# Row normalisation: another dealing of 64 KiB row chunks to partitions, in groups of four

## Chip, cores, metric

One core of a Trainium2 chip. The metric is device time in microseconds. Before: 82.85 us (median of the six runs, 82.76 to 83.07; the first three alone gave 82.86). Differences here, e12's apart, are about 1% or less, so the argument rests on the packet records of the traces (start, duration and size of every DMA packet) as much as on times.

## The reference

```python
def setup_inputs():
    batch, dim = 1024, 4096
    return {"x": np.random.randn(batch, dim).astype(np.float32), "axis": -1, "eps": np.float32(1e-12)}

def reference(x, axis, eps):
    norm = np.sqrt(np.sum(x ** 2, axis=axis, keepdims=True) + eps)
    return (x / norm).astype(np.float32)
```

16.8 MB are read and 16.8 MB written; every row is divided by its length.

## The kernel before

Two tiles of 128 partitions; each partition holds four whole rows, 64 KiB in one piece. Both loads are issued at once (at 0.00 and 0.80 us in the trace), the first even ahead of the program's opening barrier. Each tile's rows are squared into scratch, summed to norms, then scaled in place, and the tile is stored as one transfer.

```python
    R = 4
    # ... assert cut ...
    n_tiles = N // (P * R)                                            # 2
    x_t = x.rearrange("(t p r) d -> t p (r d)", p=P, r=R)
    out_t = out_flat.rearrange("(t p r) d -> t p (r d)", p=P, r=R)
    # ... pools, eps, scratch cut ...
    for i in range(n_tiles):
        g = RowGroups(nc, io, stats, scratch, D, R, eps_t)
        load = nc.sync.dma_start(out=g.flat(), in_=x_t[i])
        if i == 0:
            first_load_to_front(nc, load.ins)
        groups.append(g)

    for i, g in enumerate(groups):
        g.square_dve(R - 1)
        # ... squares, norms and scales of the four rows, cut ...
        g.square_act(2)
        g.norm(2)
        g.scale(2)
        store = nc.sync.dma_start(out=out_t[i], in_=g.flat())
    one_barrier_behind_last_store(nc, store.ins)
```

Of the kernel before, what the change touches and what calls it, by code (L numbers as in the profile page):

```python
# [1 line left out]

# [4 lines left out]


ACT_F = mybir.ActivationFunctionType
ALU = mybir.AluOpType  # L10
F32 = mybir.dt.float32


class RowGroups:


    def __init__(self, nc, io, stats, scratch, D, R, eps_t):
        self.nc = nc
        self.P = nc.NUM_PARTITIONS
        self.R = R  # L20
        self.D = D
        self.eps_t = eps_t
        self.scratch = scratch
        self.x = io.tile([self.P, R, D], F32, name="xt")
        self.ssq = stats.tile([self.P, R], F32, name="ssq")
        self.rstd = stats.tile([self.P, R], F32, name="rstd")

    def flat(self):
        return self.x.rearrange("p r d -> p (r d)")

    def square_act(self, r):
        sq_a = self.scratch["act"]
        self.nc.scalar.activation(  # L33
            out=sq_a,
            in_=self.x[:, r],
            func=ACT_F.Square,
            accum_out=self.ssq[:, r : r + 1],
        )

    def square_dve(self, r):  # L40
        sq_v = self.scratch["dve"]
        self.nc.vector.scalar_tensor_tensor(  # L42
            out=sq_v,
            in0=self.x[:, r],
            scalar=1.0,
            in1=self.x[:, r],
            op0=ALU.mult,
            op1=ALU.mult,
            accum_out=self.ssq[:, r : r + 1],
        )  # L50

    def norm(self, r, n=1):
        self.nc.scalar.activation(  # L53
            out=self.rstd[:, r : r + n],
            in_=self.ssq[:, r : r + n],
            func=ACT_F.Sqrt,
            bias=self.eps_t,
        )
        self.nc.vector.reciprocal(  # L59
            out=self.rstd[:, r : r + n], in_=self.rstd[:, r : r + n]  # L60
        )

    def scale(self, r):
        self.nc.vector.tensor_scalar_mul(  # L64
            out=self.x[:, r], in0=self.x[:, r], scalar1=self.rstd[:, r : r + 1]
        )


def first_load_to_front(nc, load):






    def move(program):
        blocks = program.main_func.blocks
        entry = blocks[0].instructions
        if any(i.name == load.name for i in entry):
            return  # L80
        body = next(
            b.instructions
            for b in blocks
            if any(i.name == load.name for i in b.instructions)
        )
        at = next(n for n, i in enumerate(body) if i.name == load.name)
        assert not body[at].sync_info.on_wait
        before = next(
            n
            for n, i in enumerate(entry)  # L90
            if i.engine == mybir.EngineType.SP and isinstance(i, mybir.InstDrain)
        )
        entry.insert(before, body.pop(at))

    nc.at_finalize(move)


def one_barrier_behind_last_store(nc, store):






    SP, POOL = mybir.EngineType.SP, mybir.EngineType.Pool

    def waits(i):
        return i.sync_info.on_wait if i.sync_info is not None else []

    def move(program):  # L110
        sem = store.sync_info.on_update[0].id
        tail = program.main_func.blocks[-1].instructions

        def take(which):
            at = next(n for n, i in enumerate(tail) if which(i))
            return tail.pop(at)

        def place(instructions, which):
            at = max(n for n, i in enumerate(tail) if which(i))
            tail[at:at] = instructions  # L120

        arrivals = [
            n
            for n, i in enumerate(tail)
            if i.engine == SP and isinstance(i, mybir.InstDrain)
        ]
        if any(w.id == sem for w in waits(tail[arrivals[-2]])):
            return
        everything = take(
            lambda i: i.engine == SP and any(w.id == sem for w in waits(i))  # L130
        )
        place([everything], lambda i: i.engine == SP and isinstance(i, mybir.InstDrain))
        reset = take(
            lambda i: i.engine == POOL
            and isinstance(i, mybir.InstDrain)
            and i.is_reset_sema
        )
        clear = take(lambda i: i.engine == POOL and isinstance(i, mybir.InstISA))
        place(
            [reset, clear],  # L140
            lambda i: i.engine == POOL and isinstance(i, mybir.InstEventSemaphore),
        )

    nc.at_finalize(move)


@with_exitstack
def kernel(
    ctx: ExitStack,
    tc: tile.TileContext,  # L150
    x: bass.AP,
    axis: bass.AP,
    eps: bass.AP,
    out: bass.AP,
):
    nc = tc.nc
    P = nc.NUM_PARTITIONS

    assert isinstance(axis, int) and axis in (-1, len(x.shape) - 1)
    eps = float(eps)  # L160

    x = x.flatten_outer_dims()
    out_flat = out.flatten_outer_dims()
    N, D = x.shape
    R = 4
    assert N % (P * R) == 0
    n_tiles = N // (P * R)
    x_t = x.rearrange("(t p r) d -> t p (r d)", p=P, r=R)
    out_t = out_flat.rearrange("(t p r) d -> t p (r d)", p=P, r=R)

    io = ctx.enter_context(tc.tile_pool(name="io", bufs=n_tiles))
    scratch_pool = ctx.enter_context(tc.tile_pool(name="scratch", bufs=1))
    stats = ctx.enter_context(tc.tile_pool(name="stats", bufs=n_tiles))

    eps_t = scratch_pool.tile([P, 1], F32)
    nc.vector.memset(eps_t, eps)  # L176
    sq_act = scratch_pool.tile([P, D], F32)
    sq_dve = scratch_pool.tile([P, D], F32)
    scratch = {"act": sq_act, "dve": sq_dve}

    groups = []
# [9 lines that stand above are left out]
        g.square_act(0)  # L191
        g.norm(0)
        g.scale(0)
        g.square_act(1)
        g.norm(1)
        g.norm(R - 1)
        g.scale(1)
        g.scale(R - 1)
# [7 lines that stand above are left out]
# [1 line left out]
_INS = ['x', 'axis', 'eps']  # L207
_OUTS = [((1024, 4096), 'float32')]

_NUMBERS = {'axis': -1, 'eps': 9.999999960041972e-13}  # L210


# [26 lines left out]
```

## Time and profile before

| | before |
|---|---|
| time, median | 82.85 us |
| span of the profiled execution | 81.13 us |
| VectorE / ScalarE busy | 28.6 / 26.4 us |
| DMA queue, share of 16 engines' span | 97.1% |
| big packets | 512 of 64 KiB, mostly 2.418 us |

In the trace before, all packets but the first sixteen start within 0.004 us of the end of another, so sixteen are under way at a time. A **round** below is the n-th packet of each of the 16 DMA engines; the trace doesn't name engines, so I sort the packets by start and take sixteen at a time. Rounds 0 to 7 are load 0, 8 to 15 load 1, 16 to 23 store 0, 24 to 31 store 1. The lines of the profile that carry the bound are in the prediction.

### The profile page before, as it was taken

The page shows a single profiled execution, that of the slowest core. Times are in us where ns is not written, and L with a number is a line of the kernel's source. Part 1 is how long each engine was busy: PE and PEld are TensorE (multiplying, and loading weights), DVE is VectorE, ACT ScalarE, POOL GpSimd, SP SyncE. Part 2 cuts the span into 40 slices and gives each one's busy share as a digit, 9 for nine tenths or more (in the row PEclk, how much of TensorE's full clock was granted, in tenths as well). Part 3 has the DMA queues.
Part 4 walks back from the last instruction along what each step waited for, and adds up shares of the span by engine and source line. Part 5 has one row for each costly group of instructions (what it writes and reads, how often), then busy time and mean ns, then how long its engine had stood idle before and what let it go on. Part 6 is the DMA issues. An engine that isn't in the chain of part 4 may idle for free.

```text
span 81.1 us, 93 instructions
## 1 busy us (share of the span) xinstructions
DVE 28.6 (35%) x21; ACT 26.4 (33%) x22; POOL 0.2 (0%) x4
## 2 busy tenths in 40 slices
DVE  0000000000199599976039995999200000000000
ACT  6000000000199999930039999950000000000000
POOL 0000000000000000000000000000000000000000
DMA  9099999299999759999099995899998399998390
GB/s 517 0 517 517 517 517 485 129 420 517 517 517 485 323 226 517 517 517 517 0 517 517 517 452 226 355 517 517 517 485 388 162 517 517 517 517 388 162 485 0
DMA packets 577, 33.55 MB, mean 414 GB/s; under 512 B 65, under 2 KB 65, under 8 KB 65
## 3 DMA queue, kind: packets, MB, share of 16 engines
q1 hardware_dynamic: 576, 33.55, 97.1%
q14 instruction: 1, 0.00, 0.0%
HBM read 16.78 MB, written 16.78 MB: 414 GB/s over the span
## 4 chain that ended last, share of the span: by engine, by line
DMA 51%; ACT 10%; DVE 9%; issue 0%
DMA xt<-in_x_dram 51%; ACT sq_act L33 9%; DVE xt L64 9%; ACT rstd L53 1%; DVE rstd L59 0%
## 5 line engine op out<-in xcount | busy, mean ns | idle before, releaser
L33 ACT ACTIVATE sq_act<-xt 128x4096 f32<-128x4096 f32 x6 | 21.6, 3608 | 26.5 <-DMA xt<-in_x_dram 26.5
L64 DVE TENSOR_SCALAR xt<-xt,rstd 128x4096 f32<-128x4096 f32 x8 | 18.8, 2353 | 0.3
L42 DVE SCALAR_TENSOR_TENSOR sq_dve<-xt 128x4096 f32<-128x4096 f32 x2 | 8.9, 4426 | 25.0 <-DMA xt<-in_x_dram 25.0
L53 ACT ACTIVATE rstd<-ssq,eps_t 128x1 f32<-128x1 f32 x8 | 2.1, 288 | 0.1
L59 DVE RECIPROCAL rstd<-rstd 128x1 f32<-128x1 f32 x8 | 1.3, 159 | 2.4 <-ACT rstd L53 2.4
L33 ACT ACT_TABLE_LOAD x1 | 1.3, 1283 | 0.8 <-PEq L220 0.8
L53 ACT ACT_TABLE_LOAD x1 | 1.3, 1283 | 0.0
L33 ACT ACTIVATION_READ_ACCUMULATOR sq_act<-xt 128x1 f32 x6 | 1.1, 186 | 0.0
L176 DVE MEMSET eps_t<- 128x1 f32 x1 | 0.1, 59 | 0.9 <-PEq L220 0.9
L42 DVE DVE_READ_ACCUMULATOR sq_dve<-xt 128x1 f32 x2 | 0.2, 83 | 0.0
L220 POOL MEMSET const-uint8-127<- 128x1 uint8 x1 | 0.1, 102 | 0.0
L220 POOL MEMSET const-bfloat16-1.0<- 128x1 bf16 x1 | 0.1, 101 | 0.0
L220 POOL MEMSET const-float32-0.0<- 128x1 f32 x1 | 0.1, 98 | 0.2 <-issue 0.2
L220 POOL MEMSET const-float32-1.0<- 128x1 f32 x1 | 0.1, 98 | 0.0
## 6 DMA issues: line engine op xcount, KB each, us to landing
xt<-in_x_dram SPq DMA_DIRECT2D x2, 31.5
out_dram<-xt SPq DMA_DIRECT2D x2, 23.3
```

The source lines that it names most:

```text
L33: self.nc.scalar.activation(out=sq_a, in_=self.x[:, r], func=ACT_F.Square, accum_out=self.ssq[:, r : r + 1],)
L42: self.nc.vector.scalar_tensor_tensor(out=sq_v, in0=self.x[:, r], scalar=1.0, in1=self.x[:, r], op0=ALU.mult, op1=ALU.mult, accum_out=self ...
L53: self.nc.scalar.activation(out=self.rstd[:, r : r + n], in_=self.ssq[:, r : r + n], func=ACT_F.Sqrt, bias=self.eps_t,)
L59: self.nc.vector.reciprocal(out=self.rstd[:, r : r + n], in_=self.rstd[:, r : r + n])
L64: self.nc.vector.tensor_scalar_mul(out=self.x[:, r], in0=self.x[:, r], scalar1=self.rstd[:, r : r + 1])
L176: nc.vector.memset(eps_t, eps)
L220: nc = _bacc.Bacc("TRN2", target_bir_lowering=False, num_devices=1)
```

## The change

Intent: packets that are under way at the same time should read and write neighbouring 64 KiB chunks. Whether they do is not shown, since no record names a packet's partition or address. Before, partition p holds chunk p of its tile; after, partition 4g + b holds chunk 32b + g.

```diff
-    x_t = x.rearrange("(t p r) d -> t p (r d)", p=P, r=R)
-    out_t = out_flat.rearrange("(t p r) d -> t p (r d)", p=P, r=R)
+    B = 4
+    x_t = x.rearrange("(t b g r) d -> t g b (r d)", b=B, g=P // B, r=R)
+    out_t = out_flat.rearrange("(t b g r) d -> t g b (r d)", b=B, g=P // B, r=R)
```

## The prediction

> **What bounds the kernel now.** I read the page's strip of 40 slices and its queue table first, then the chain of waits, then the timeline around the four DMA issues and the DMA sequencer's own waits, and last the single packet records in the trace.
>
> The page, parts 1 to 3 (a digit of the DMA row is the mean busy share of the 16 DMA engines in a fortieth of the span; an 8 or 0 between 9s is mostly packets counted in a neighbouring slice):
>
> ```profile
> DVE 28.6 (35%) x21; ACT 26.4 (33%) x22; POOL 0.2 (0%) x4
> DMA  9099999299999759999099995899998399998390
> GB/s 517 0 517 517 517 517 485 129 420 517 517 517 485 323 226 517 517 517 517 0 517 517 517 452 226 355 517 517 517 485 388 162 517 517 517 517 388 162 485 0
> DMA packets 577, 33.55 MB, mean 414 GB/s; under 512 B 65, under 2 KB 65, under 8 KB 65
> q1 hardware_dynamic: 576, 33.55, 97.1%
> ```
>
> See that both compute engines work a third of the time, while the packets of one queue fill 97.1% of what 16 DMA engines have in the span. The 576 packets are 512 of 64 KiB (one for each partition of each of four transfers) and 64 of 4 bytes, the 16 completion marks of each transfer.
>
> The chain that ended last (start, length, what):
>
> ```profile
> 0.80 41.09 DMA xt<-in_x_dram
> 41.91 3.72 ACT sq_act L33 x2
> 54.89 2.35 DVE xt L64
> ```
>
> and the two store issues in the timeline, with the DMA sequencer's waits below:
>
> ```profile
> 37.88 0.35 SPq L202 DMA_DIRECT2D out_dram<-xt  x1
> 57.27 0.34 SPq L202 DMA_DIRECT2D out_dram<-xt  x1
> SPq L202 <- DVE xt L64: 31.3, 2, 15.9
> SPq L234 <- DMA out_dram<-xt: 22.5, 2, 19.3
> ```
>
> The chain says load, compute, and then stops at the last scale, so a beginner would credit 15 us of it to compute. The packet records correct that. All packets of one engine follow each other without a hole, 32 to an engine, in the order load 0, load 1, store 0, store 1, eight each. The first starts at 1.02 us and the last ends at 80.24 us. Store 0's last packets start at 57.75 to 58.50 us and end at 60.17 to 60.92 us, and store 1 was issued at 57.27 us: some 2.9 us before the first DMA engine needed it. So compute on tile 1 is hidden behind store 0 with nearly 3 us to spare, and compute on tile 0 (21.9 to 37.9 us) behind load 1. **The span is one unbroken stream of DMA packets.**
>
> The length of that stream: 441 of the 512 big packets take 2.418 to 2.420 us. 32 x 2.418 = 77.38 us would be the stream at that pace; the mean packet is 2.460 us, so the real sum is 78.71 us. The excess of 1.33 us is in two places: the first packet of each engine averages 3.10 us (0.68 us over), and the last four rounds of load 1 average 2.48, 2.47, 2.44 and 2.92 us (together 0.64 us over). 1.02 + 78.71 + about 0.5 us by which the engines' starts are staggered is 80.24; then some 0.9 us for the last completion and the end makes the span of 81.13, and the timed 82.86 us are 1.73 us more than the span.
>
> [...]65,536 B in 2.418 us is 27.1 GB/s for one engine, 433.7 GB/s for 16.[...]
>
> **The change part by part.** It alters the DRAM side of four transfers and nothing else. A tile is 8 MiB, 128 chunks of four rows, 64 KiB each. Before, partition p holds chunk p. After, partition 4g + b holds chunk 32b + g.
> - *Packets and bytes.* A partition still holds one contiguous 64 KiB chunk: 128 packets for each transfer, 512 in all, at 2.418 us. Change: 0.
> - *Compute.* Each partition still has four whole rows, so the 6 squares of 3608 ns, 2 squares of 4426 ns and 8 scales of 2353 ns are the same instructions. Change: 0. Load and store use the same mapping, so the result is right.
> - *Issue.* Still two loads and two stores from one queue, 0.33 to 0.38 us each. The DRAM side now has one more dimension (32 x 4 x 16384 in place of 128 x 16384). Were each issue half as long again, that is 0.2 us; only load 0 pays it openly, the others are issued behind running packets. Change: 0 to +0.2 us, I take +0.05.
> - *Engines.* [...]
> - *Addresses in flight.* This is what the change is for. [...] What this can win is only time above 2.418 us, of which there is 1.33 us. The 0.68 us of the first round is start-up and should stay. Of the 0.64 us in load 1, 0.50 is in the very last round, which falls where store 0 is issued (37.88 us); I take it for the meeting of load and store, which stays. The other 0.14 us (0.064 + 0.049 + 0.023) [...]might go. Change: -0.14 to 0; I take -0.05.
>
> Sum: 0 + 0 + 0.05 + 0 - 0.05 = 0. The prediction is 82.8 us, practically the time before.
>
> **The rivals.**
> 1. *The engine split loses its order.* [...] Estimate from the trace: packets of some 4.8 us, a stream of about 155 us, a time of about 160 us. For it: the two sides no longer have the same form. [...] Chance about 0.07. [...]
> 2. *HBM dislikes the new pattern.* [...] If every packet were 5% slower (2.54 us), the stream would be 3.9 us longer, the time 86.7 us. Chance about 0.05.
> 3. *HBM likes it.* [...]all 0.64 us go: 82.2 us, 0.8% less. If the first round were also perfect, 1.33 us: 81.5 us, 1.6% less, still within 2%. For it: slow rounds exist at all. Against: 24 of 32 rounds have nothing to win. I give a visible gain of 0.3 us or more a chance of 0.2, a gain over 2% (below 81.2 us) nearly none, since the floor by this sum is 81.5.
> 4. *Compute surfaces.* It would have to end 2.9 us later for a hole between the stores. Load 1 ends at the same time and compute is unchanged, so this needs rival 1 or 2 first. Chance about 0.
>
> **Range and chances.** The same stream gives 82.6 to 83.1, as the three runs before scatter by 0.23 us. Down to 82.0 holds rival 3 in its likely size; up to 83.6 holds a slower issue or a few slow rounds. Outside lie rivals 1 and 2, 0.12 together, mostly over 2%. So faster 0.02, same 0.86, slower 0.12.
>
> **What would show each step right or wrong.** Right: 576 packets in the queue again, 64 completion marks, big packets at 2.418 us, a queue share near 97%, compute groups with the same means, store 1 issued near 57.3 us before store 0 ends. The first packet at 1.0 us shows the issue cost (1.2 us would be the dearer one). Load 1's last rounds tell whether the addresses mattered: 2.92 us again in the last one means that store 0's start did it; 2.42 means it was the addresses. Wrong: a packet mean near 4.8 us[...], or all packets a few per cent longer, most in the loads or most in the stores (HBM)[...].

Where a cut is marked, something stood that no trace of this case shows. The sum came to 0, and so the prediction to 82.8 us. The term for the engines stood at 0 because of a rule for dividing a transfer among them; in the term for the addresses (-0.05) the 1.33 us above 2.418 us that it rests on are measured. That 2.418 us can't be beaten is the estimate from the trace before, where no packet is shorter and 441 of 512 last at most 2.420 us. The 4.8 us of rival 1 is 2.418 us doubled, and the 5% of rival 2 an assumption; why either should come about is cut. The completion marks are measured: in the trace before, sixteen packets of 4 bytes lie at the end of each transfer, the last of them at 21.54, 41.59, 60.91 and 80.23 us.

## The result, and the profile after

| | before | after |
|---|---|---|
| time, median of 6 | 82.85 us | 83.15 us (83.10 to 83.27) |
| ratio of fast runs | | 1.0034, 95% interval 1.0018 to 1.0050 |
| span of the profiled execution | 81.13 us | 81.4 us |

Ratios are the mean time of one kernel's fast runs over that of the other's of the same rounds, so not quite the ratio of the medians quoted. The time is the same within 2%, inside the predicted range, and slower by 0.3 us, clear of noise in these rounds; timed again on another chip (e9) the ratio was 1.0024, with an interval that just touches 1.

The page after: the DMA row (busy tenths of the 16 engines in 40 slices), the packet count and the queue.

```profile
DVE 28.6 (35%) x21; ACT 26.4 (32%) x22; POOL 0.2 (0%) x4
DMA  9099993999993899995899999399999489999560
DMA packets 577, 33.55 MB, mean 412 GB/s; under 512 B 65, under 2 KB 65, under 8 KB 65
q1 hardware_dynamic: 576, 33.55, 96.2%
```

Same packets and bytes, same compute, one percentage point less of the engines' span filled. The chain after, and the DMA sequencer's waits:

```profile
1.31 40.81 DMA xt<-in_x_dram
42.15 3.72 ACT sq_act L33 x2
55.12 2.35 DVE xt L64
SPq L203 <- DVE xt L64: 31.3, 2, 15.9
SPq L235 <- DMA out_dram<-xt: 22.0, 2, 19.3
```

The chain has the same links. Two things differ: the load piece, which begins with the issue of load 1, starts at 1.31 instead of 0.80 us, and compute on tile 1 starts only 0.24 us later (42.15 for 41.91). Of 0.5 us lost there, half has come back by then. The two issues that matter stand in the timeline. The first load (start, length), before and then after:

```profile
0.00 0.38 SPq L184 DMA_DIRECT2D xt<-in_x_dram  x1
```

```profile
0.00 0.67 SPq L185 DMA_DIRECT2D xt<-in_x_dram  x1
```

The start of compute on each tile, which is the landing of its load (bracket: idle before it, and what ended the idling), before:

```profile
21.91 3.62 ACT L33 ACTIVATE sq_act<-xt 128x4096 f32<-128x4096 f32 x1 [19.83 <-DMA xt<-in_x_dram]
41.91 3.62 ACT L33 ACTIVATE sq_act<-xt 128x4096 f32<-128x4096 f32 x1 [6.64 <-DMA xt<-in_x_dram]
```

and after, with the store issue between:

```profile
22.70 3.62 ACT L33 ACTIVATE sq_act<-xt 128x4096 f32<-128x4096 f32 x1 [20.10 <-DMA xt<-in_x_dram]
38.67 0.61 SPq L203 DMA_DIRECT2D out_dram<-xt  x1
42.15 3.62 ACT L33 ACTIVATE sq_act<-xt 128x4096 f32<-128x4096 f32 x1 [6.09 <-DMA xt<-in_x_dram]
```

Load 0 lands 0.79 us later than before, but load 1 follows it after 19.45 us instead of 20.00. Eight packets of 2.418 us are 19.34 us: load 1 used to lose some 0.6 us, and no longer does.

The packet records let the end of the stream be written as a sum of four parts along the last engine of each round:

| part (us) | before | after | difference |
|---|---|---|---|
| start of the first packet | 1.02 | 1.44 | +0.41 |
| from there to the latest engine's second packet (round 1) | 3.60 | 3.98 | +0.38 |
| from there to the latest start of round 16 (rest of both loads) | 36.97 | 36.41 | -0.56 |
| from there to the end of the last packet (both stores) | 38.63 | 38.66 | +0.03 |
| end of the last packet | 80.24 | 80.49 | +0.26 |

So the small difference is two losses at the start and one gain, most of it in the last round of load 1: round 15 averaged 2.921 us before and 2.438 us after. Each is questioned below, with these four parts as the measure. One trace of each kernel is not enough for the sizes: the second traces (e1 and e8) give +0.42, +0.20, -0.42 and +0.01, +0.22 us in all, with the same signs.

### The profile page after: what moved, and what is told of

Same layout as the page of the kernel before. It is cut to its first block, busy times and chain, and to the rows that moved or that the text cites. A ratio compares the mean times of both kernels' runs of the same rounds, so it can differ in the third digit from the quotient of the medians.

```text
span 81.4 us, 93 instructions
## 1 busy us (share of the span) xinstructions
DVE 28.6 (35%) x21; ACT 26.4 (32%) x22; POOL 0.2 (0%) x4
## 3 DMA queue, kind: packets, MB, share of 16 engines
q1 hardware_dynamic: 576, 33.55, 96.2%
## 4 chain that ended last, share of the span: by engine, by line
DMA 50%; ACT 10%; DVE 9%; issue 0%
DMA xt<-in_x_dram 50%; ACT sq_act L33 9%; DVE xt L64 9%; ACT rstd L53 1%; DVE rstd L59 0%
## 5 line engine op out<-in xcount | busy, mean ns | idle before, releaser
L33 ACT ACTIVATE sq_act<-xt 128x4096 f32<-128x4096 f32 x6 | 21.6, 3608 | 26.2 <-DMA xt<-in_x_dram 26.2
L64 DVE TENSOR_SCALAR xt<-xt,rstd 128x4096 f32<-128x4096 f32 x8 | 18.8, 2353 | 0.3
L42 DVE SCALAR_TENSOR_TENSOR sq_dve<-xt 128x4096 f32<-128x4096 f32 x2 | 8.9, 4426 | 24.8 <-DMA xt<-in_x_dram 24.8
```

What stands on the lines that cost most here:

```text
L33: self.nc.scalar.activation(out=sq_a, in_=self.x[:, r], func=ACT_F.Square, accum_out=self.ssq[:, r : r + 1],)
L42: self.nc.vector.scalar_tensor_tensor(out=sq_v, in0=self.x[:, r], scalar=1.0, in1=self.x[:, r], op0=ALU.mult, op1=ALU.mult, accum_out=self ...
L64: self.nc.vector.tensor_scalar_mul(out=self.x[:, r], in0=self.x[:, r], scalar1=self.rstd[:, r : r + 1])
```

## The experiments

Twelve kernels. The lengths of the issues prompted several of them. With one plain stride on both sides (128 rows of 16384) the kernel before takes 0.33 to 0.38 us for each of its issues; the changed kernel, with 32 x 4 x 16384 on the DRAM side, takes 0.57 to 0.67 us. A switch of the builder, set in the diffs of e2 and e5, makes the issue of the plain pattern longer too (0.56 us for load 0 in e2, 0.55 us for store 0 in e5); what else it does is not shown. I call an issue of 0.33 to 0.39 us the short form and one of 0.55 us or more the long form.

### e1: the kernel before, once more

> The kernel before, once more, for a second trace. In the first trace the last four rounds of load 1 (16 packets each) were slow: the mean packet of that transfer was 2.498 us against 2.418 us in the stores. If that belongs to the kernel, it is there again: mean 2.47 to 2.53 us, the last packet ending near 80.2 us. If it was an accident of one execution, the mean is below 2.43 us and the last packet ends near 79.7 us.

82.70 us (one run). Last packet ends at 80.01 us, load 1's mean packet 2.460 us: a little under the range that I wrote for it, still far from 2.43. Rounds 12 to 14 averaged 2.423, 2.419 and 2.418 us; in the first trace they were 2.482, 2.467 and 2.441. So those three slow rounds were an accident of one execution. Round 15 is slow again, 2.745 us on average: that belongs to the kernel.

### e2: old addresses, long issue

```diff
     nc = _bacc.Bacc("TRN2", target_bir_lowering=False, num_devices=1)
+    nc.dge_precook = False
```

> The kernel before with its addresses, but its four transfers issued without the short form[...]. Theory A (the changed kernel loses time by its issue and wins it back by its addresses): first issue 0.67 us instead of 0.38, first packet at 1.44 us instead of 1.02, second round starting at 5.4 us at the latest engine instead of 4.6, and load 1 still slow (mean near 2.50): 83.6 us, 0.9% over before. Theory B (the slow rounds of load 1 depend on when the engines run against each other, not on the addresses): the same late start, but load 1 near 2.42: 83.15 us, as the changed kernel. Theory C (the late start comes from the addresses): issue longer, but first round as before: 82.9 to 83.1 us.

82.85 us, ratio 1.0014 (0.9992 to 1.0036). The first issue in its timeline:

```profile
0.00 0.56 SPq L184 DMA_DIRECT2D xt<-in_x_dram  x1
```

First packet at 1.36 us, so 0.34 us of the 0.41 are the loss of the short form. The second part is 3.69 us, as before. Round 15 averages 2.446 us with not one address changed: theory A (the addresses mend load 1) falls. Theory B named the time as that of the changed kernel, 83.15; it is 0.3 us less, and in the traces it is the changed kernel's longer second part (3.98 us) that is missing here. Note that e2 also puts store 0 in the long form, so it doesn't tell timing from form; e5 and e6 do that.

### e3: tile 0 as before, tile 1 dealt

"Dealt" is the mapping of the changed kernel.

```diff
-    x_t = x.rearrange("(t p r) d -> t p (r d)", p=P, r=R)
-    out_t = out_flat.rearrange("(t p r) d -> t p (r d)", p=P, r=R)
+    B = 4
+    plain = "(t p r) d -> t p (r d)"
+    dealt = "(t b g r) d -> t g b (r d)"
+    dims = {plain: {"p": P}, dealt: {"b": B, "g": P // B}}
+    HOW = (plain, dealt)
+    x_t = [x.rearrange(h, r=R, **dims[h])[i] for i, h in enumerate(HOW)]
+    out_t = [out_flat.rearrange(h, r=R, **dims[h])[i] for i, h in enumerate(HOW)]
```

> Tile 0 as before, tile 1 as in the changed kernel. Theory A: the first packet starts at 1.02 us as before, load 1's packets average 2.42 us, and the time is 0.54 us below before: 82.3 us, ratio 0.9935; this would beat both. Theory B (timing between engines, not addresses): start as before, load 1 slow as before, mean near 2.50: 82.85 us.

82.90 us, ratio 1.0010 (0.9988 to 1.0033): theory B's number. Load 1 has the new addresses, and its round 15 is as slow as ever, 2.917 us. Its landing and the (short) store issue:

```profile
37.90 0.35 SPq L207 DMA_DIRECT2D out_dram<-xt  x1
41.88 3.62 ACT L33 ACTIVATE sq_act<-xt 128x4096 f32<-128x4096 f32 x1 [6.59 <-DMA xt<-in_x_dram]
```

### e4: short issue, other addresses

```diff
-    x_t = x.rearrange("(t p r) d -> t p (r d)", p=P, r=R)
-    out_t = out_flat.rearrange("(t p r) d -> t p (r d)", p=P, r=R)
+    x_t = x.rearrange("(p t r) d -> t p (r d)", p=P, r=R)
+    out_t = out_flat.rearrange("(p t r) d -> t p (r d)", p=P, r=R)
```

> Short issue kept (one stride on the DRAM side), other addresses: partition p of tile t holds chunk 2p + t, [...]tile 0 and tile 1 share the whole 16 MiB. If load 1's slow rounds come from particular addresses of its last quarter, they go or move: with load 1 near 2.42 us the time is 82.3 us. If wider steps are worse for HBM, load packets are longer than 2.45 us throughout and the time is 83 us or more. If the slow rounds belong to that moment of the program whatever the addresses, they stay in rounds 12 to 15 and the time is 82.85 us.

82.75 us, ratio 0.9994 (0.9973 to 1.0014). Rounds 1 to 14 run at 2.418 to 2.419 us, round 15 at 3.012. The last alternative holds for round 15: with these addresses too, the slow round belongs to a moment of the program. After these four, what set round 15 apart was store 0: short in every trace with a slow round 15, long in the two without.

### e5: only store 0 in the long form

```diff
+        nc.dge_precook = i > 0
         store = nc.sync.dma_start(out=out_t[i], in_=g.flat())
+        nc.dge_precook = True
```

> The kernel before, with only store 0 issued in the long form; both loads and store 1 keep the short form, all addresses as before. So far the last load packet of each engine was stretched by 0.33 to 0.59 us in all four traces with a short store 0, and by 0.02 to 0.03 us in both with a long one. Theory A2 (the form of store 0's issue does it): first packet at 1.02 us, round 15 near 2.44 us, last packet ends near 79.7 us, time about 82.4 us, 0.5% below before and below both kernels. Theory B2 (only the moment of the issue does it; this one comes as early as before): round 15 stays at 2.75 to 3.0 us, time 82.85 us.

82.41 us, ratio 0.9937 (0.9921 to 0.9953), against 82.98 us before on that chip.

```profile
37.88 0.55 SPq L203 DMA_DIRECT2D out_dram<-xt  x1
41.36 3.62 ACT L33 ACTIVATE sq_act<-xt 128x4096 f32<-128x4096 f32 x1 [6.09 <-DMA xt<-in_x_dram]
```

The store is issued at the same moment as before (37.88), its issue takes 0.55 us instead of 0.35, and load 1 lands 0.55 us earlier (41.36 for 41.91). Round 15 averages 2.490 us: most of the stretch has gone, but five of its sixteen packets still have 0.12 to 0.27 us over 2.418. So A2 is near the truth, but that the form alone decides is not what e5 shows: a longer issue is also a later one.

### e6: store 0 short, 0.8 us later

```diff
         g.scale(2)
+        if i == 0:
+            part = g.x[:, 2, :1024]
+            nc.vector.tensor_scalar_mul(out=part, in0=part, scalar1=1.0)
         store = nc.sync.dma_start(out=out_t[i], in_=g.flat())
```

> The kernel before, all short forms, store 0 issued about 0.6 us later (a multiplication by 1.0 over a quarter of one row stands before it), near 38.5 us and so as late, against the start of round 15, as in the changed kernel. Theory A2 (form): round 15 still stretched to 2.7 to 3.0 us, time 82.85 us. Theory B2 (moment): round 15 near 2.44 us, time about 82.4 us.

82.33 us, ratio 0.9930 (0.9908 to 0.9952): faster than before by doing useless work.

```profile
38.68 0.34 SPq L205 DMA_DIRECT2D out_dram<-xt  x1
41.37 3.62 ACT L33 ACTIVATE sq_act<-xt 128x4096 f32<-128x4096 f32 x1 [6.03 <-DMA xt<-in_x_dram]
```

Round 15 averages 2.435 us with the short form. A2 falls as the whole story: a short store that comes late enough stretches next to nothing. Nor is the moment (B2) the whole story, since e5 kept the moment and lost most of the stretch. e1 and e2 say the same: same addresses, store 0 issued on average 0.16 and 0.13 us before the packets of round 15 start, and the excess is 0.33 us with the short form, 0.03 with the long. Both count. Packet by packet, in the five traces with a short store 0 up to here (80 packets of round 15): of the 62 that started after the issue, or at most 0.1 us before it, each lasted 0.11 to 0.88 us over 2.418; of the 14 that had started 0.3 us or more before it, none lasted more than 0.02 us over.

### e7: tile 0 dealt, tile 1 as before

The diff is that of e3 with `HOW = (dealt, plain)`.

> Tile 0 as in the changed kernel, tile 1 as before: the other half of the run with tile 1 dealt, which was as fast as before. If the whole cost sits in load 0's issue and the whole return in store 0's form, this is the changed kernel's time: 83.15 us, first packet at 1.44 us, round 15 near 2.44 us. If tile 1's long forms also cost, it is nearer to 82.85 us.

83.04 us, ratio 1.0016 (0.9998 to 1.0035): between the two numbers, and the interval just holds 1. The trace is clearer: first packet 1.44 us, second part 3.89 us, round 15 2.426 us, last packet ends at 80.23 us, which is also where the changed kernel's second trace (e8) ends. All three differences come with tile 0.

### e8: the changed kernel once more

> The changed kernel once more, for a second trace: first packet at 1.44 us, round 15 below 2.46 us. The point in question is the first round: in its first trace it averaged 3.26 us and the second round began over 1.0 us of spread, with the last engine at 5.42 us. If this belongs to the kernel the last engine starts its second packet between 5.25 and 5.55 us again; if it was chance, near 5.1 us, as with the long issue on the old addresses.

82.92 us (one run). First packet 1.43 us, latest second packet 5.33 us, round 15 2.424 us. The slow start belongs to the kernel.

### e9 and e10: the long form with a third dimension, on two sets of addresses

e9 is the changed kernel, timed again. e10 keeps its form and changes the addresses:

```diff
-    x_t = x.rearrange("(t b g r) d -> t g b (r d)", b=B, g=P // B, r=R)
-    out_t = out_flat.rearrange("(t b g r) d -> t g b (r d)", b=B, g=P // B, r=R)
+    x_t = x.rearrange("(g t b r) d -> t g b (r d)", b=B, g=P // B, r=R)
+    out_t = out_flat.rearrange("(g t b r) d -> t g b (r d)", b=B, g=P // B, r=R)
```

> The changed kernel again, timed on the same chip as the next one, as its yardstick: 82.9 to 83.2 us, first packet at 1.44 us, last engine's second packet at 5.3 to 5.45 us.

> The changed kernel's instruction form (third dimension, long issue) with other addresses: partition 4g + b of tile t holds chunk 8g + 4t + b[...]. The long issue on old addresses without a third dimension had its first packet at 1.36 us and the last engine's second packet at 5.05 us; the changed kernel 1.44 and 5.33 to 5.42 us. If the third dimension costs these 0.3 us, they are here too: last engine at 5.3 us or later, time equal to the changed kernel's run beside it within 0.1 us. If its addresses cost them, this run shows about 5.05 us and is 0.2 to 0.3 us faster than the changed kernel.

e9: 83.03 us, ratio to before 1.0024 (1.0000 to 1.0049). e10: 82.66 us, ratio 0.9984 (0.9962 to 1.0005). The means of six runs differ by 0.35 us (83.04 and 82.69), though the first issue is nearly as long:

```profile
0.00 0.65 SPq L185 DMA_DIRECT2D xt<-in_x_dram  x1
```

e10's first packet starts at 1.41 us (e9: 1.43), so the third dimension costs 0.05 to 0.08 us over e2's 1.36. The second part is 3.60 us in e10 and 3.89 in e9. Over all traces of the dealing in fours and its relatives it separates cleanly: 3.57 to 3.70 us in the nine traces whose load 0 has other addresses, 3.89 to 3.98 in the four whose load 0 is dealt as in the changed kernel. So it is the new addresses that cost some 0.3 us at the latest engine, in the first round; my first alternative falls, the second holds. One caution: e10's profiled execution (82.90 us) was the slowest of its six, so its trace, whose stream ends only 0.14 us before e9's, doesn't show where all of the 0.35 us between the times lies.

### e11: store 0 one microsecond earlier (wrong result)

Only half of the last scale of tile 0 is done, so the output is wrong there.

```diff
-        g.scale(2)
+        if i > 0:
+            g.scale(2)
+        else:
+            part = g.x[:, 2, :2048]
+            nc.vector.tensor_scalar_mul(out=part, in0=part, scalar1=g.rstd[:, 2:3])
```

> The kernel before with short forms, but only half of the last scale of tile 0 (a wrong result on purpose: half a row group is not normalised), so that store 0 is issued near 36.7 us, over 1.2 us before the last load packets start. In the traces so far every last load packet that started before, or less than 0.1 us ahead of, a short store issue... more exactly: of a short issue at most 0.1 us after the packet's start was stretched (0.11 to 0.88 us), none over 0.3 us after it by more than 0.02 us. Theory B2 in its wide form (any store that is there before the packet is under way stretches it): round 15 at 2.75 to 3.0 us again, 82.85 us. In its narrow form (only a store that arrives while the packet starts): no stretch in round 15 and perhaps one in round 14, which starts near 35.5 us; if none at all, the time is 82.3 us.

83.10 us, ratio 1.0034 (1.0010 to 1.0059): slower than before, with less work.

```profile
36.76 0.35 SPq L206 DMA_DIRECT2D out_dram<-xt  x1
42.06 3.62 ACT L33 ACTIVATE sq_act<-xt 128x4096 f32<-128x4096 f32 x1 [6.85 <-DMA xt<-in_x_dram]
```

Round 14, under way when the store arrives, stays at 2.420 us. Round 15, the last before the store, averages 3.327 us, more than I expected. The wide form holds: it is the last load packet that is stretched when a (short) store waits behind it at its start, by 0.91 us on average here, by 0.33 to 0.59 us where the store is issued around that start (the four traces before, e1, e3, e4), by 0.02 us where it comes 0.2 to 0.7 us later (e6).

### e12: groups of eight

```diff
-    B = 4
+    B = 8
```

> The changed kernel with groups of eight partitions in place of four (16 groups of 8). The rival of the prediction that engines lose their order: [...]packets take up to 4.8 us, time up to 160 us. [...]2.42 us packets and 82.9 to 83.3 us.

(So two outcomes: packets of up to 4.8 us, which is 2.418 us doubled, and up to 160 us if the rival holds; 2.42 us and 82.9 to 83.3 us if not. The reasons given for either are cut, as no trace shows them.)

158.4 us (one run), correct. The page:

```profile
DMA  9993999299984999199929999789999799999950
DMA packets 576, 33.55 MB, mean 214 GB/s; under 512 B 64, under 2 KB 64, under 8 KB 64
q1 hardware_dynamic: 576, 33.55, 96.9%
```

The same packets on all 16 engines (the queue fills 96.9% of their span), at half the rate: load packets average 5.05 us. This is about the time that the prediction's first rival gives. What doubles the packets is not shown, and one thing doesn't fit a plain doubling: the first two rounds of store 0 ran at 2.59 and 2.42 us.

## Why the prediction was right in the time, and where its steps failed

- **Bound, packets, bytes, compute: right.** (One count was off: 27 of the 32 rounds, not 24, ran at 2.418 to 2.419 us before. What sets this pace, 433.7 GB/s for 16 engines, is not shown; no run tests it.) 576 packets, 2.418 us, and square and scale means of 3608, 4426 and 2353 ns after as before. Both stores took 38.63 to 38.68 us in every trace but e12's.
- **Engines: right in the outcome, the argument not shown.** All 16 engines stayed in use (the queue fills 96.2% of their span, 97.1% before) with packets of 2.418 us; e12 shows what was at stake, load packets of 5.05 us. The argument rested on a rule for dividing a transfer among engines that no record shows. "Chance about 0.07" for that rival was an honest guess, not knowledge.
- **Issue: the size was wrong.** "Change: 0 to +0.2 us, I take +0.05." The issue took 0.28 us more and the first packet came 0.41 us later: 0.34 for the long form (e2) and the rest with the third dimension. I had seen one added dimension, and missed that the plain pattern had a shorter form to lose.
- **Addresses in flight: the sign was wrong.** "Change: -0.14 to 0." The 0.14 us in rounds 12 to 14 was an accident (e1). The new addresses cost about 0.3 us in the first round (e9 against e10) and nothing after it: from round 1 on, loads and stores run at 2.418 us, round 15 aside, on every set of addresses tried, e12's groups of eight apart. Why only the first round is dearer stays open.
- **Round 15: cause half seen, consequence wrong.** "I take it for the meeting of load and store, which stays." It is that meeting, and it went. And the sign that I named for telling the causes apart, "2.42 means it was the addresses", was wrong: with the new addresses and a short store at the old moment the round stayed slow (e3), with the old addresses and a later store it became fast (e6). In the changed kernel load 0 lands 0.79 us later, so store 0 is issued 0.79 us later, but round 15 starts later too (earliest engine 38.25 for 38.03 us, latest 39.23 for 38.50). In its three traces (after, e8, e9) the store is issued 0.00 to 0.20 us before the packets of round 15 start on average, much as in e1 (0.16), where a short store stretched them by 0.33 us; here the excess is 0.01 to 0.02 us. So the later start alone doesn't account for the gain; the long form of store 0 does most of it, as in e5, which had it at the old moment. No run has the late start with a short store 0.
- **The sum.** Predicted 0; measured +0.41 + 0.38 - 0.56 + 0.03 = +0.26 us in the traces, +0.30 us in the medians. The figure near zero was luck: missed losses and a missed gain nearly cancelled. "Same" within 2% was safer than that, since the two losses alone, 0.79 us, are 1.0%; but without the gain the time would have been near 83.7 us, just past the predicted range.

**What stays open.** What the DMA engine does when a store waits behind its last load packet; the runs show when it costs and how much, not how. Nor why the form counts: by the packet rule of e6, a short store issued up to 0.1 us after a packet's start stretches it, yet where store 0 was long (112 packets of round 15 in seven traces), the median excess is 0.01 us and the largest 0.38, even with packets that started up to 0.6 us after the issue. The first packets of a long load 0 come 0.34 us later too (e2); whether a long store 0 is likewise later than its issue no trace shows.

## What to carry to other kernels

Where one unbroken stream of DMA packets is the span, the places to look are its start and its turn from loads to stores: here a plain 128-row pattern on both sides was worth 0.34 us on the first load, and a store 0 that came 0.8 us later (e6), or at the old moment in the long form (e5), was worth some 0.6 us in all. These two, 0.6 to 0.7% below the kernel before, are the best versions found. An access pattern that looks equivalent may change the form of the issue (0.38 us for load 0 before, 0.67 us after), so compare the issue's length in the timeline before reasoning about addresses. And read a second trace before explaining a slow stretch of the first.
